# One hybrid block on one core: down sums added to the residual at once, modulation loads moved, T4 halves packed two to a tile

## The chip, the cores and the metric

The kernel runs on one core of a Trainium2 chip. The metric is the device time of one execution in microseconds; the number quoted for a kernel is the median of its runs. A profile is one further execution, with its own time.

## The reference

One layer (DEPTH is 1) of a diffusion backbone block. 512 latent tokens and 256 context tokens of width 2048; the output is the latent stream after a final RMSNorm. Cut to what matters:

```python
mod = (c_act @ w_mod + b_mod)                        # 2048 x 12288
sh1, sc1, gt1, sh2, sc2, gt2 = split(mod, 6)
h  = rmsnorm(x, g_norm1) * (1 + sc1) + sh1           # the same for ctx
lat_in, lat_gates = project_heads(h, w_in, ...)      # 4 GLA heads, 4 mLSTM heads
(lat_gla, lat_ml) = recurrent_groups(lat_in, ctx_in) # both directions
x = x + gt1 * merge_groups(lat_gla, lat_ml, lat_gates, ..., w_out)
h2 = rmsnorm(x, g_norm2) * (1 + sc2) + sh2
u_gate, u_val = split(h2 @ w_up, 2)                  # D_FF = 5504 each
g = conv3x3_depthwise(u_gate on an 8 x 64 grid) + conv_b
x = x + gt2 * ((silu(g) * u_val) @ w_down)
return rmsnorm(x, g_final)
```

Everything is in float32.

## The kernel before

The kernel is written in a tile framework: the program states operations on named tiles, and a planner places them on the engines' queues by priority (`tc.high_priority()`) and readiness, gives out buffers by tag and sets the semaphores. A tile asked for with a tag that is in use waits until the tile that had it has been read for the last time, wherever in the program that read stands. Blocks marked `pinned`, and single instructions marked `keep_in_program_order`, stay in the order of the program. Activations lie transposed, features on the partitions and 512 tokens along the free axis. Each float32 product is made of three matmuls of a high and a low part (`mm3`); every loaded weight tile is split for that by `split_new`: ACT casts `hi`, DVE subtracts to get `lo`. PE, DVE, ACT and the DMA queues run beside each other.

The stages in order:

1. `project_first`: the norm, the first two of the six modulation regions, and the projections of the first two heads.
2. For each head `h`, `weave` runs the stages of head `h` between the projection steps of head `h + 1` (`project_steps`). At the end of the last GLA head, while the first mLSTM head (index `H`, 4) is projected, `ml_gates` computes the gate rows of all mLSTM heads: a chain of small matmuls, DVE scans and the total `cum`, which PE then transposes into `pa`.
3. The four gates (`unit` on `w_gates`, tiles `ga`), then `w_out` (tiles `wo`), in 8 steps `kp` each. The new residual `x2` is also stored to DRAM tiles `x2d`.
4. The MLP in 11 groups `q` of `QUADS` (3, then ten times 4) blocks of 128 features. For each group: `up_gate`, `convolve`, `up_val`, and one group later `down_sums`, four blocks of 512 outputs each.
5. The last group's down blocks, the final norm and the output.

**Modulation fillers.** Regions 2 to 5 of the modulation vector (four totals `n` each, 16 in all) are computed on DVE, in `mod_chunk`: one load of 512 KB on SP's queue and two DVE instructions, eight chunks to a total; `mod_sums` and `mod_end` close a total with small pinned matmuls on PE (tiles `mr`, `mc`). These are put in a list `fillers`; every weight load calls `fill()`, which adds `rate[0]` to a credit and runs as many fillers as it allows. All must have run by the end of `w_out`. `project_steps` sets the rate to 2 from step 3 for heads `h >= H`; the first gate has 1.5; the rest of the gates and `w_out` have 2.0.

**The groups 1 to 10** use a two-by-two product in seven multiplications (`seven`, `four`). It needs sums of token halves: `token_sums(j)` makes, from the pair of tiles `x2[2j]` and `x2[2j+1]`, the operands `bt` (three halves), and leaves a fourth difference, T4, in a half of one of the two tiles. `token_last(j)` later splits that T4 into `bq[j][:, 1, :]`, which is the space of a half of `h2` that group 0, computed without the sums, still reads to the end of its `up_val`. The `x2` tiles have the tags `y0` to `y15`, and these tags are used again: by the convolutions `cv` of group 0, by the products `gh`, `gl` that go into the down blocks, and by `u`, `v`, `t` in `four` and `up_val`.

**Down sums.** A block's four sums go through ACT into a tile `st` (three buffers) and from there by a GpSimd-issued DMA to DRAM, accumulating there. With `FOLD = NQ - 3 = 8`, the groups up to 8 go unscaled into a separate total `dacc`, the first of them as plain stores. After the down blocks of group 8, `fold()` loads each of the 16 tiles of `dacc`, scales it on ACT by the gate `modc[5]` and adds it to `x2d`. Group 9 is scaled when it is copied and goes straight to `x2d`; group 10 is added on chip.

The order of the calls at the start of stage 4:

```python
for j in reversed(range(3, KP)):
    token_sums(j)
up_val(0, convolve(0))
for j in range(3):
    token_sums(j)
for j in range(KP):
    token_last(j)
down_sums(0, (0, 1), True)
```

Names as the profile has them: `ug`, `uv`, `dn`, `dl` are the accumulators of `up_gate`, `up_val`, the down blocks and the last ones; `hi_d` and `lo_d`, `hi_aug`, `hi_bug`, `hi_auv`, `hi_buv` and their `lo` are the split weights; `sum_m` is a modulation total, and `raw_...` a loaded weight tile.

Of the kernel before, what the change touches and what calls it, by code (L numbers as in the profile page):

```python
# [11 lines left out]
F32 = mybir.dt.float32  # L12
F32R = mybir.dt.float32r
U8 = mybir.dt.uint8
AF = mybir.ActivationFunctionType
ALU = mybir.AluOpType
PSUM = bass.MemoryType.PSUM

P = 128
HW = 256  # L20
D = 2048
KT = D // P
KP = KT // 2
T = 512
# [3 lines left out]
H = 4  # L28
# [8 lines left out]
LEVELS = [1, 2, 4, 8, 16, 32, 64]  # L37
QUADS = [3] + [4] * 10
NQ = len(QUADS)
FOLD = NQ - 3  # L40
GLA_COLS = {"q": 0, "k": 512, "v": 1024, "g": 2048, "lr": 3072}
ML_COLS = {"q": 3088, "k": 3600, "v": 4112, "g": 5136, "lr": 6160}

# [28 lines left out]
def block_kernel(ctx: ExitStack, tc: tile.TileContext, a: dict, out: bass.AP):  # L72
    nc = tc.nc
    V, S, G, PE = nc.vector, nc.scalar, nc.gpsimd, nc.tensor

    def pool(stack, name, bufs=1, space=None, waits="pool"):
        if space is None:
            return stack.enter_context(tc.tile_pool(name=name, bufs=bufs, reuse_waits=waits))
        return stack.enter_context(tc.tile_pool(name=name, bufs=bufs, space=space, reuse_waits=waits))

    def sub(o, x, y):
        V.tensor_tensor(out=o, in0=x, in1=y, op=ALU.subtract)  # L82
# [7 lines left out]
    def split(hi, lo, x):  # L90
        S.copy(hi, x)  # L91
        return V.tensor_tensor(out=lo, in0=x, in1=hi.bitcast(F32), op=ALU.subtract).ins  # L92
# [24 lines left out]
    modc = {n: keep.tile([P, KT], F32, name=f"mod{n}") for n in (2, 3, 4, 5)}  # L117
# [24 lines left out]
    def acc(name, shape=(P, T)):  # L142
        return (banks8[0] if banks8 else psA).tile(list(shape), F32, name=name, tag="acc")
# [5 lines left out]
    def ytile(k, name, shape=(P, T), dtype=F32):  # L149
        return yp.tile(list(shape), dtype, name=name, tag=f"y{k}")  # L150
# [14 lines left out]
    fillers = []  # L165
    rate, credit = [0], [0]
# [21 lines left out]
    def load_split(src, name, n=2, w=512):  # L188
        raw = load_raw(src, name, n, w)
        with tc.high_priority():  # L190
            parts = split_new(raw, name, (n, w))
        fill()
        return parts
# [34 lines left out]
    def unit(src, name, xh, xl, n=4, late=False, rates=None):  # L228

        accs = [acc(f"{name}_{i}") for i in range(n)]  # L230
        for _ in unit_steps(src, name, xh, xl, accs, late, rates):
            pass
        return accs
# [130 lines left out]
    def project_steps(h, banks):  # L364

        for kp in range(KP):
            rate[0] = 2 if h >= H and kp >= 3 else 0
            wh, wl = load_split(a["w_heads"][h, kp], f"h{h}_{kp}")
            for g in range(6):
                project_chunk(kp, wh, wl, banks[g], g)  # L370
                yield (1.36, 1.36, 1.44, 1.44, 1.04, 1.04)[g]
# [122 lines left out]
    cv = xp.tile([P, 32], F32, name="cv")  # L494
# [76 lines left out]
    for c0, n, hs, m in ((0, T, hx, gm[0]), (T, TC, hc, gm[1])):  # L571
        ps = psb(f"gm{c0}", (P, n))
        for k in range(KT):
            g = 32 * (k % 4)
# [417 lines left out]
    for h in range(1, 2 * H):  # L992
        if h + 1 < 2 * H:
            accs = [acc(f"a{h + 1}_{g}", BANKS[g]) for g in range(6)]
            steps = project_steps(h + 1, accs)
        else:
            rate[0] = 1.5
            accs = [acc(f"ga0_{i}") for i in range(4)]
# [12 lines left out]
    gp = pool(st_3, "gp", 2)  # L1011
    rp = pool(st_3, "rp")
    mod_raw.append(pool(st_3, "mraw3", 4, waits="tile"))
    rate[0] = 2.0
    for g in range(4):
        if g:
            accs = unit(a["w_gates"][g], f"ga{g}", *hx)
        for i in range(4):
            k = 4 * g + i
# [50 lines left out]

    dram = ctx.enter_context(tc.tile_pool(name="dram", bufs=1, space=bass.MemoryType.DRAM))
    x2d = [dram.tile([P, T], F32, name=f"x2d{k}", tag=f"x{k}") for k in range(KT)]
    dacc = [dram.tile([P, T], F32, name=f"dacc{k}", tag=f"d{k}") for k in range(KT)]
    sums2 = []
    for n in range(4):
        pinned[0] = n == 3
        accs = unit(a["w_out"][n], f"wo{n}", yh, yl)
# [9 lines left out]
        _, r2 = token_rstd(sums2, rp, "rms2", idle=4)  # L1087
        idle_products(acc("idle", (P, P)), sums2[0][:, 0:P], 7)
    pinned[0] = False
    print("LEFT", len(fillers))  # L1090
    assert not fillers
    st_3.close()
    st_h.close()
# [7 lines left out]
    stp = pool(ctx, "stp", 3, waits="tile")  # L1101
# [4 lines left out]
    def flat(x):  # L1106
        return x.rearrange("p a b -> p (a b)")

    bq = [[operand(j, part, "q", f"bq{part}{j}", (P, 4, HW)) for j in range(KP)] for part in "hl"]
# [10 lines left out]
    def half(k, i):  # L1120
        return x2[k][:, HW * i : HW * i + HW]

    def token_sums(j):

        k0, k1 = 2 * j, 2 * j + 1
        for k in (k0, k1):
            S.activation(x2[k], x2[k], AF.Identity, bias=modc[3][:, k : k + 1])
        sub(half(k0, 0), half(k0, 1), half(k0, 0))
        sub(half(k0, 1), half(k0, 1), half(k1, 1))
        sub(half(k1, 1), half(k1, 1), half(k0, 0))  # L1130
        sub(half(k1, 0), half(k1, 1), half(k1, 0))
        split(flat(bt[0][j][:, 0:2, :]), flat(bt[1][j][:, 0:2, :]), x2[k0])
        split(bt[0][j][:, 2, :], bt[1][j][:, 2, :], half(k1, 1))

    def token_last(j):

        split(bq[0][j][:, 1, :], bq[1][j][:, 1, :], half(2 * j + 1, 0))

    cwt = fp.tile([P, NF, 9], F32, name="cwt")
    cbt = fp.tile([P, 152], F32, name="cbt")[:, 0:NF]  # L1140
# [52 lines left out]
    def convolve(q):  # L1193
        convs = []
        for i in range(QUADS[q]):
            f = first_f(q) + i
            t = ytile(8 + i if q == 0 else 8 + 2 * i, f"cv{f}")
            t3 = t.rearrange("p (r c) -> p r c", c=GW)
            for tap in range(9):
                src = pads[:, i, tap // 3 : tap // 3 + ROWS, tap % 3 : tap % 3 + GW]  # L1200
                w = cwt[:, f, tap : tap + 1]
                if tap == 0:
                    S.activation(t3, src, AF.Identity, scale=w, bias=cbt[:, f : f + 1])  # L1203
                else:
                    V.scalar_tensor_tensor(out=t3, in0=src, scalar=w, in1=t3, op0=ALU.mult, op1=ALU.add)  # L1205
            S.activation(t, t, AF.Silu)
            convs.append(t)
        return convs

    def up_val(q, convs):  # L1210

        def product(i):
            if q == 0:
                gh, gl = (ytile((11, 12, 13, 14, 15, 7)[2 * i + n], f"g{p}{i}", dtype=F32R) for n, p in enumerate("hl"))
            elif q == NQ - 1:
                gh, gl = (operand(4 + i, p, "t", f"g{p}{first_f(q) + i}", (P, T)) for p in "hl")
            else:
                gh, gl = (ytile(2 * i + n, f"g{p}{first_f(q) + i}", dtype=F32R) for n, p in enumerate("hl"))
            split(gh, gl, convs[i])
            gs[first_f(q) + i] = (gh, gl)  # L1220

        if q == 0:
            accs = unit(a["w_up3"][1], "uv0", *h2, n=3)
            with tc.high_priority():
                for i, ps in enumerate(accs):
                    mul(convs[i], convs[i], ps)
                    product(i)
        else:
            def put(mh, th, x, ps, op):
                t = ytile(13, f"t{q}_{mh}{th}", (P, 2, HW))  # L1230
                V.tensor_tensor(out=t, in0=x, in1=ps, op=op)  # L1231
                for i in range(2):
                    c = convs[2 * mh + i][:, HW * th : HW * th + HW]
                    mul(c, c, t[:, i, :])
                if (mh, th) in ((1, 1), (0, 1)):
                    for i in range(2):
                        product(2 * mh + i)

            four(seven(a["w_up4"][2 * q - 1], f"uv{q}"), f"uv{q}", put)
# [16 lines left out]
    def down_sums(q, blks, by_f=False):  # L1256

        for blk in blks:
            accs = down_block(q, blk, by_f and blk == blks[0])
            with tc.high_priority():  # L1260
                for i in range(4):
                    k = 4 * blk + i
                    t = stp.tile([P, T], F32, name=f"st{q}_{k}", tag="st")
                    S.activation(t, accs[i], AF.Copy, scale=modc[5][:, k : k + 1] if q > FOLD else 1.0)  # L1264
                    if q == 0:
                        nc.gpsimd.dma_start(dacc[k], t)
                    else:
                        nc.gpsimd.dma_start(x2d[k] if q > FOLD else dacc[k], t, accum_op=ALU.add)  # L1268

    def fold():  # L1270

        for k in range(KT):
            t = stp.tile([P, T], F32, name=f"fold{k}", tag="st")
            nc.gpsimd.dma_start(t, dacc[k])
            S.activation(t, t, AF.Copy, scale=modc[5][:, k : k + 1])
            nc.gpsimd.dma_start(x2d[k], t, accum_op=ALU.add)

    up_gate(0)
    st_p.close()
    banks8.append(pool(ctx, "psM", 8, PSUM, waits="tile"))  # L1280
    for j in reversed(range(3, KP)):
        token_sums(j)
    up_val(0, convolve(0))
    for j in range(3):
        token_sums(j)
    for j in range(KP):
        token_last(j)
# [1 line left out]
    for q in range(1, NQ):  # L1289
        up_gate(q)  # L1290
        down_sums(q - 1, (2, 3) if q == 1 else range(3) if q == NQ - 1 else range(4))
        if q - 1 == FOLD:
            fold()
        up_val(q, convolve(q))
    down_sums(NQ - 2, (3,))

# [1 line left out]
    q = NQ - 1  # L1298
# [16 lines left out]
    for blk in range(3):  # L1315
        accs = down_block(q, blk)
# [38 lines left out]
    for hf, sl in enumerate(halves):  # L1355
        accs = [acc(f"dl{hf}_{i}", (P, T // 2)) for i in range(4)]
# [3 lines left out]
        for at, (n, i) in enumerate(order):  # L1360
# [5 lines left out]
            gh, gl = gs[fs[n]]  # L1366
# [76 lines left out]
```

## Time and profile before

| what | us |
|---|---|
| median of 3 runs | 2571.09 |
| lowest and highest run | 2570.16, 2573.83 |
| the profiled execution's own time | 2568.5 |
| its span | 2566.8 |
| PE busy in the span | 2487.4 |
| DVE busy | 1816.0 |
| ACT busy | 1021.1 |
| mean granted TensorE clock | 0.989 |

How to read the profile: the span runs from the first to the last instruction of the program. Engines are PE (matmul), PEld (weight load, beside PE), DVE, ACT, POOL and SP. A group's row has the line of the kernel, the engine, the operation, what it writes and reads, the count, then busy time, mean ns of one, and the idle time before it with what ended it. A row of waits reads "who waited <- for whom: us in total, times, longest". A row of windows has the stretch (us from the start of the span), its length, busy time of each engine with the count, the granted clock as a share of full speed, the mean busy share of the 16 DMA engines, and GB/s. Ends of matmuls are modelled, so a busy PE is not PE at its peak.

### The profile page before, as it was taken

Reading aid. Unit: us, or ns where it says so; the run is one execution under the profiler, and the core shown is the slowest. Engines: PE = TensorE matmul, PEld = TensorE weight load, DVE = VectorE, ACT = ScalarE, POOL = GpSimd, SP = SyncE. Lnnn points to the kernel's source line nnn. Section 1 sums busy time; section 2 is a strip of 40 time slices with the busy share of each in tenths; the row PEclk is TensorE's granted clock in tenths of the full one; section 3 lists DMA queues with packets and bytes.
Section 4 is the critical chain, followed back from the end, with each engine's and each line's share of the span. In section 5 each row is a group of like instructions: output and inputs, shape, how many; then the busy total and the mean of one; then the engine's idle time right before and its main releaser. Section 6 shows DMA issues by size and latency. Waiting matters only on the chain. (4 is left out here: it accounts for less than half of the span.)

```text
span 2566.8 us, 39444 instructions
## 1 busy us (share of the span) xinstructions
PE 2487.4 (97%) x15740; PEld 2218.3 (86%) x15740; DVE 1816.0 (71%) x2880; ACT 1021.1 (40%) x1530; POOL 200.5 (8%) x274
## 2 busy tenths in 40 slices
PE   6999999999999999999899999999999999998898
PEld 4887899788987888888798999999999999987897
DVE  6566764644446877749679787878787878784786
ACT  4225543322223233227344444444444444443445
POOL 0000000000000000000000101010111101014022
PEclk9999999999999999999999999999999999998999
DMA  9741111323334878732343736464655555468474
GB/s 384 266 166 34 34 42 42 123 83 107 115 124 159 281 270 303 255 128 89 123 136 95 168 109 163 112 155 122 148 128 143 132 140 135 128 150 198 117 193 132
DMA packets 124113, 380.59 MB, mean 148 GB/s; under 512 B 14421, under 2 KB 18841, under 8 KB 123929
## 3 DMA queue, kind: packets, MB, share of 16 engines
q1 hardware_dynamic: 94680, 318.29, 36.9%
q0 software_dynamic: 28160, 58.73, 12.3%
q8 instruction: 123, 2.02, 0.3%
q10 hardware_dynamic: 1088, 1.05, 0.1%
q14 instruction: 62, 0.50, 0.1%
HBM read 323.49 MB, written 54.53 MB: 147 GB/s over the span
## 5 line engine op out<-in xcount | busy, mean ns | idle before, releaser
L97 PE MATMUL dn<-gh,hi_d 128*128 128x512 f32 x672 | 262.2, 390 | 11.0 <-ACT gh L91 11.0
L97 PE MATMUL dn<-gl,hi_d 128*128 128x512 f32 x672 | 262.3, 390 | 0.0
L97 PE MATMUL dn<-gh,lo_d 128*128 128x512 f32 x672 | 262.0, 390 | 0.0
L1205 DVE SCALAR_TENSOR_TENSOR cv<-pads,cwt,cv 128x512 f32<-128x512 f32 x344 | 239.6, 744 | 1.1 <-ACT cv L1203 0.3
L305 DVE SCALAR_TENSOR_TENSOR sum_m<-raw_m,csil,sum_m 128x512 f32<-128x512 f32 x240 | 179.9, 750 | 8.7 <-DMA raw_m<-in_w_mod 3.2
L92 DVE TENSOR_TENSOR lo_buv<-sum_uv,hi_buv 128x1024 fp32r<-128x1024 f32 x80 | 97.9, 1223 | 122.3 <-ACT hi_buv L91 122.3
L1268 POOL DMA_DIRECT2D dacc<-st x128 | 111.8, 922 | 886.9 <-ACT st L1264 884.0
L97 PEld LDWEIGHTS dn<-gh,hi_d 128*128 128x128 f32 x672 | 126.6, 188 | 37.6 <-ACT gh L91 11.4
L97 PE MATMUL a<-hi_h,hTh 128*128 128x256 f32 x512 | 151.0, 295 | 0.5 <-ACT e L398 0.5
L97 PEld LDWEIGHTS dn<-gh,lo_d 128*128 128x128 f32 x672 | 126.4, 188 | 26.7 <-DVE lo_d L92 0.5
L97 PEld LDWEIGHTS dn<-gl,hi_d 128*128 128x128 f32 x672 | 126.5, 188 | 26.5 <-DVE gl L92 0.8
L97 PE MATMUL ug<-bth,hi_bug 128*128 128x256 f32 x480 | 137.3, 287 | 8.5 <-DVE u_uv L82 7.1
L97 PE MATMUL a<-lo_h,hTh 128*128 128x256 f32 x512 | 145.3, 284 | 0.0
L97 PE MATMUL a<-hi_h,hTl 128*128 128x256 f32 x512 | 145.2, 284 | 0.0
L97 PE MATMUL uv<-bth,hi_buv 128*128 128x256 f32 x480 | 137.8, 287 | 6.4 <-ACT hi_buv L91 6.4
L97 PE MATMUL uv<-bqh,hi_auv 128*128 128x256 f32 x480 | 136.7, 285 | 3.4 <-ACT hi_auv L91 3.4
L97 PE MATMUL uv<-bth,lo_buv 128*128 128x256 f32 x480 | 137.9, 287 | 1.2 <-DVE lo_buv L92 1.2
L92 DVE TENSOR_TENSOR lo_d<-raw_d,hi_d 128x1024 fp32r<-128x1024 f32 x86 | 102.7, 1195 | 50.5 <-ACT hi_d L91 49.8
L91 ACT CAST hi_d<-raw_d 128x1024 fp32r<-128x1024 f32 x86 | 88.7, 1031 | 123.9 <-PE ug L97 71.1
L97 PE MATMUL uv<-btl,hi_buv 128*128 128x256 f32 x480 | 137.4, 286 | 0.0
L97 PE MATMUL uv<-bqh,lo_auv 128*128 128x256 f32 x480 | 136.8, 285 | 0.2 <-DVE lo_auv L92 0.2
L97 PE MATMUL ug<-bqh,hi_aug 128*128 128x256 f32 x480 | 136.1, 284 | 0.7 <-DVE t L1231 0.4
(384 smaller groups left out, 7408.6 us busy)
## 6 DMA issues: line engine op xcount, KB each, us to landing
raw_m<-in_w_mod SPq DMA_DIRECT2D x192, 512.0 KB, 5.0
raw_d<-in_w_down SPq DMA_DIRECT2D x82, 512.0 KB, 3.4
raw_ug<-in_w_up SPq DMA_DIRECT2D x80, 512.0 KB, 3.6
raw_uv<-in_w_up SPq DMA_DIRECT2D x80, 512.0 KB, 5.2
dacc<-st POOLq DMA_DIRECT2D x144, 256.0 KB, 5.3
raw_h<-in_w_heads SPq DMA_DIRECT2D x64, 512.0 KB, 3.6
raw_ga<-in_w_gates SPq DMA_DIRECT2D x32, 512.0 KB, 4.2
raw_wo<-in_w_out SPq DMA_DIRECT2D x32, 512.0 KB, 4.6
```

What stands on the lines that cost most here:

```text
L91: S.copy(hi, x)
L92: return V.tensor_tensor(out=lo, in0=x, in1=hi.bitcast(F32), op=ALU.subtract).ins
L97: ins = PE.matmul(*args, **kw)
L305: V.scalar_tensor_tensor(out=parts[0], in0=x, scalar=ck, in1=parts[0], op0=ALU.mult, op1=ALU.add)
L1205: V.scalar_tensor_tensor(out=t3, in0=src, scalar=w, in1=t3, op0=ALU.mult, op1=ALU.add)
L1268: nc.gpsimd.dma_start(x2d[k] if q > FOLD else dacc[k], t, accum_op=ALU.add)
```

## The change

Three edits.

1. `FOLD`, `dacc` and `fold()` go. Every group's down sums are scaled by `modc[5]` on ACT and added to `x2d` in DRAM by an accumulating DMA, the first group's too.
2. `project_steps` runs fillers for `h > H` in place of `h >= H`: ten fillers fewer while the first mLSTM head is projected. From the second gate to the end of `w_out` the rate is 2.2 in place of 2.0.
3. T4 of pair `j` is kept in `rest(j)`, a half of tile `4 * (j // 2) + 2`, so that two of them share one tile (2, 6, 10 and 14), in place of a half of tile `2j + 1`. The convolutions of group 0 take tiles 8, 9 and 13 in place of 8, 9 and 10; its products take 11, 12, 15, 7, 4 and 5 in place of 11, 12, 13, 14, 15 and 7. `token_sums(2)` comes between `convolve(0)` and `up_val(0)`, and of the others 1 comes before 0.

```diff
-FOLD = NQ - 3
...
-            rate[0] = 2 if h >= H and kp >= 3 else 0
+            rate[0] = 2 if h > H and kp >= 3 else 0
...
-    rate[0] = 2.0
+    rate[0] = 2.2
...
-    dacc = [dram.tile([P, T], F32, name=f"dacc{k}", tag=f"d{k}") for k in range(KT)]
...
+    def rest(j):
+
+        return half(4 * (j // 2) + 2, j % 2)
+
     def token_sums(j):
...
-        sub(half(k1, 0), half(k1, 1), half(k1, 0))
         split(flat(bt[0][j][:, 0:2, :]), flat(bt[1][j][:, 0:2, :]), x2[k0])
+        sub(rest(j), half(k1, 1), half(k1, 0))
         split(bt[0][j][:, 2, :], bt[1][j][:, 2, :], half(k1, 1))
 
     def token_last(j):
 
-        split(bq[0][j][:, 1, :], bq[1][j][:, 1, :], half(2 * j + 1, 0))
+        split(bq[0][j][:, 1, :], bq[1][j][:, 1, :], rest(j))
...
-            t = ytile(8 + i if q == 0 else 8 + 2 * i, f"cv{f}")
+            t = ytile((8, 9, 13)[i] if q == 0 else 8 + 2 * i, f"cv{f}")
...
-                gh, gl = (ytile((11, 12, 13, 14, 15, 7)[2 * i + n], f"g{p}{i}", dtype=F32R) for n, p in enumerate("hl"))
+                gh, gl = (ytile((11, 12, 15, 7, 4, 5)[2 * i + n], f"g{p}{i}", dtype=F32R) for n, p in enumerate("hl"))
...
-                    S.activation(t, accs[i], AF.Copy, scale=modc[5][:, k : k + 1] if q > FOLD else 1.0)
-                    if q == 0:
-                        nc.gpsimd.dma_start(dacc[k], t)
-                    else:
-                        nc.gpsimd.dma_start(x2d[k] if q > FOLD else dacc[k], t, accum_op=ALU.add)
-
-    def fold():
-
-        for k in range(KT):
-            t = stp.tile([P, T], F32, name=f"fold{k}", tag="st")
-            nc.gpsimd.dma_start(t, dacc[k])
-            S.activation(t, t, AF.Copy, scale=modc[5][:, k : k + 1])
-            nc.gpsimd.dma_start(x2d[k], t, accum_op=ALU.add)
+                    S.activation(t, accs[i], AF.Copy, scale=modc[5][:, k : k + 1])
+                    nc.gpsimd.dma_start(x2d[k], t, accum_op=ALU.add)
...
-    up_val(0, convolve(0))
-    for j in range(3):
+    convs = convolve(0)
+    token_sums(2)
+    up_val(0, convs)
+    for j in (1, 0):
         token_sums(j)
...
-        if q - 1 == FOLD:
-            fold()
```

More of the change, by code (lines that the diff above doesn't have):

```diff
@@ L1089, in block_kernel @@
     pinned[0] = False
-    print("LEFT", len(fillers))
     assert not fillers
```

## The prediction

> **What bounds the kernel now.** I read the page first, then PE's waits over the whole span, then the stretches where PE idles.
>
> ```profile
> span 2566.8 us, 39444 instructions
> PE 2487.4 (97%) x15740; PEld 2218.3 (86%) x15740; DVE 1816.0 (71%) x2880; ACT 1021.1 (40%) x1530; POOL 200.5 (8%) x274
> PEclk9999999999999999999999999999999999998999
> ...
> PE dn L97 <- ACT gh L91: 11.0, 1, 11.0
> PE ug L97 <- DVE u_uv L82: 8.7, 2, 7.1
> PE uv L97 <- ACT hi_buv L91: 6.4, 2, 3.9
> PE pa L102 <- DVE cum L88: 3.9, 1, 3.9
> PE uv L97 <- ACT hi_auv L91: 3.4, 1, 3.4
> ```
>
> PE is busy for 97% of the span, and the change leaves its matmuls alone. What can be won is therefore the time in which PE waits, and the time after a wait in which its clock is granted below 1. Leaving aside the start, the five waits shown are the largest, and each lies at a place that the diff touches: `dn<-gh` in the first down block (the T4 edit), `pa<-cum` in `ml_gates` (the loads edit), and `uv<-hi_buv`, `uv<-hi_auv` and `ug<-u_uv` (7.1 of its 8.7) beside `fold`. So I price each place by comparing the stage with the same stage where nothing waits.
>
> **The fold.** These are windows cut at PE's first and last matmul of a stage: `uv` of group 8, `uv` of group 9 (just after `fold`), `ug` of group 9, `ug` of group 10. Columns: length, PE busy, granted clock, DMA share, GB/s. The waits under them are of the stretch 2290 to 2410.
>
> ```profile
> 2188.77:2229.25 40.48, 40.48 (x339) 1.00 0.46 117
> 2313.14:2372.29 59.15, 47.90 (x339) 0.86 0.87 195
> 2229.09:2269.76 40.67, 40.67 (x339) 1.00 0.32 104
> 2372.12:2423.30 51.18, 43.09 (x339) 0.93 0.41 115
> ...
> ACT fold L1275 <- DMA fold<-dacc: 37.0, 11, 6.2
> DVE lo_buv L92 <- ACT hi_buv L91: 26.9, 7, 7.5
> ```
>
> The same number of matmuls takes 59.15 instead of 40.48 and 51.18 instead of 40.67: 18.67 + 10.51 = 29.2 us. The cause is in the rows: ACT takes its instructions in order, and waits 37.0 us for loads of the separate total; behind these stand the casts `hi_buv` that feed the weight splits, and, at the end, the copy that `u_uv` starts from. Part of the loss is clock (0.86 and 0.93). The diff deletes all of it: 16 loads, 16 activations, 16 accumulating stores. What is late next there is nothing that I can see: `uv` of group 8 has the same down blocks ahead of it, with the same accumulating stores, and no wait. I take the whole 29.2.
>
> What replaces it: every `st` now has the scale of `modc[5]`.
>
> ```profile
> L1264 ACT ACTIVATE st<-dn x144: 579/600/604, 1245.6 to 2316.2; 128x512 f32<-128x512 f32 x144
> L1264 ACT ACTIVATE st<-dn,mod x16: 677/690/693, 2430.2 to 2509.1; 128x512 f32<-128x512 f32 x16
> ```
>
> That is 90 ns more for each of 144, 13 us on an engine busy for 40%, in fours: 0.36 us per down block. ACT's idle time beside a block hides it; without that cover it would be 13 us. The scale itself is there in time, since all modulation work ends before the up-projection. The stores to `x2d` of different groups lie a whole group apart, so the wait of an add for the add before it on the same tile costs nothing.
>
> **The first down blocks.** `dn` of group 0 comes in two pairs of blocks with the same matmuls. Then DVE's convolution taps (all of them, and two rows of the one that runs last), and the engines (PE, PEld, DVE, ACT, POOL, clock, DMA) in `uv` of group 0, the first pair, and `ug` of group 1.
>
> ```profile
> 1226.05:1255.74 29.69, 18.71 (x75) 0.83 0.41 141
> 1295.89:1312.73 16.84, 16.80 (x76) 1.00 0.63 211
> ...
> L1205 DVE SCALAR_TENSOR_TENSOR cv<-pads,cwt,cv 128x512 f32<-128x512 f32 x344 | 239.6, 744 | 1.1 <-ACT cv L1203 0.3
> 1222.70 1.54 DVE L1205 SCALAR_TENSOR_TENSOR cv<-pads,cwt,cv 128x512 f32<-128x512 f32 x2 [0.28 <-ACT cv L1203]
> 1234.98 3.10 DVE L1205 SCALAR_TENSOR_TENSOR cv<-pads,cwt,cv 128x512 f32<-128x512 f32 x4
> ...
> 1158.00:1226.00 68.00, 66.64 (x298) 55.04 (x298) 67.34 (x121) 49.77 (x81) 0.00 (x0) 1.00 0.26 82
> 1226.00:1255.74 29.74, 18.76 (x75) 14.53 (x75) 16.51 (x25) 10.52 (x16) 2.97 (x6) 0.83 0.41 141
> 1255.57:1296.05 40.48, 40.48 (x338) 40.47 (x337) 24.89 (x34) 14.77 (x18) 1.52 (x3) 1.00 0.32 105
> ```
>
> The first pair loses 29.69 - 16.84 = 12.85 us, 11.0 of it one wait for `gh`. One convolution starts only at 1222.70, since its tile (y9) holds a T4 half until `token_last` has written it into the space of `h2`, which `uv` reads to its end. The new `rest` keeps all T4 halves in tiles 2, 6, 10 and 14, and the convolutions take 8, 9 and 13, which are free by the time the taps can run. So the third convolution moves ahead of `uv`'s end, and `token_sums(1)`, `token_sums(0)` and the `token_last` move behind it.
>
> Is there room on DVE? Before 1226 it is full (67.34 of 68), and of the late convolution's 8 taps the first 2 run before 1226, so 6 taps moved ahead (6 x 0.744 = 4.5 us) push as much other work behind. Behind, 16.51 us of work would stand in 16.84 us: just full, then 15.6 us free in `ug`. What is queued behind the moved sums is the split of the first `ug` weights, and PE waits for that. Bounds: 0, if the order lets the splits go first, to 3 us, one such set of splits late. I take 1.0, nearer to 0, as `ug` needs the sums of one pair per 5 us only.
>
> The other cost is DMA. The first 16 stores were plain and now add. The software queue's rows of 1240 to 1320 (16 plain) and 1400 to 1450 (16 adding), then the landing times, plain and adding:
>
> ```profile
> q0 software_dynamic: 1268, 4.20, 14.3%
> q0 software_dynamic: 2304, 4.20, 53.6%
> DMA to landing us min/median/max: 2.3/4.2/7.0
> DMA to landing us min/median/max: 3.8/5.4/10.9
> ```
>
> One plain store takes 0.143 x 80 / 16 = 0.72 us of all 16 engines, one that adds 0.536 x 50 / 16 = 1.68; 8 of them per pair add 7.7 us. The first pair then needs 0.41 x 29.69 + 7.7 = 19.9 us of DMA in 16.84, the second 0.63 x 16.84 + 7.7 = 18.3: 3.1 and 1.5 us overdue. There are 3 `st` buffers, so a late landing holds ACT, and behind it the casts for the next weights. Upper bound 3.1 + 1.5, plus 1.2 of later landing at each pair: 7.0 us. Lower bound 0, since the loads that compete are partly for a stage with a share of 0.32 and can slip; below 0 is excluded, an add being the dearer in both rows. I take the middle, 3.5. [...]
>
> Sum: 12.85 - 1.0 - 3.5 = 8.35 us.
>
> **The modulation loads.** `h > H` takes 10 chunks (20 DVE instructions, 10 loads of 512 KB on SP) out of the stage in which `ml_gates` runs; they move into the stretch of gates and `w_out`, where the rate goes from 2.0 to 2.2. First DVE between 486 and 515, then PE's second wait there, then the same engine columns as above.
>
> ```profile
> L305 DVE SCALAR_TENSOR_TENSOR sum_m<-raw_m,csil,sum_m 128x512 f32<-128x512 f32 x12 | 9.0, 748 | 2.3 <-DMA raw_m<-in_w_mod 2.1
> PE pgc L97 <- DVE dg L866: 1.1, 2, 0.9
> 510.00:515.00 5.00, 1.09 (x11) 0.90 (x10) 4.96 (x6) 0.60 (x1) 0.00 (x0) 0.80 0.42 116
> 515.00:520.00 5.00, 4.06 (x23) 3.73 (x22) 3.36 (x8) 0.27 (x2) 0.00 (x0) 0.52 0.73 257
> ```
>
> These 12 stand between the links of a chain that DVE runs for `cum`, for which PE waits 3.9 us. 9.0 us out of that chain is more than twice the wait, so it goes, with 0.9 of `pgc`. The clock then is not lowered: 4.06 x 0.48 + 1.09 x 0.20 = 2.2 us. Together 7.0 us. After it nothing is late in that stage but waits of 0.3. [...]
>
> Where they go to:
>
> ```profile
> 815.00:1095.00 280.00, 280.00 (x1305) 228.20 (x1304) 213.09 (x296) 82.74 (x110) 6.82 (x9) 1.00 0.77 268
> DVE sum_m L303 <- PE mr L311: 25.4, 7, 3.7
> raw_m<-in_w_mod SPq DMA_DIRECT2D x81, 512.0 KB, 5.2
> q1 hardware_dynamic: 21313, 72.59, 74.9%
> ```
>
> PE is busy for all of the 280 us. 20 instructions at 0.75 us bring DVE from 213 to 228 us; 10 loads at 0.749 x 280 / 72.59 x 0.524 = 1.5 us bring the DMA share from 0.77 to 0.83. On SP each stands ahead of weight loads, which are four buffers ahead. Bounds of the cost: 0 (both below full) and 15 us (DVE full). Nothing can be won, as PE does not wait. I take 0: the share moves by a twentieth.
>
> **Sum.** 29.2 + 8.35 + 7.0 = 44.5 us. The profiled execution took 2568.5 us (its span, 2566.8, and 1.7 around it), so 2524.0; the median of the runs, 2571.09, lies 2.6 above, so 2526.6, which I give as 2526.5.
>
> **Rivals.** (1) The convolution is no longer late, but PE only waits a little further on: DVE, full up to 1243, and the adding stores make `ug` of group 1 late, and the convolutions of group 1 after it, a stretch which is tight already:
>
> ```profile
> 1352.88:1399.00 46.12, 42.52 (x339) 40.98 (x338) 44.05 (x69) 17.34 (x22) 0.00 (x0) 1.00 0.24 81
> ```
>
> There `ug` of group 2 takes 46.12 instead of 40.67 with DVE at 44 of 46. For it: that row. Against it: DVE's 15.6 free microseconds in `ug` of group 1, in between. All 8.35 us would go: 2535.
>
> (2) `cum` is not what holds `pa`: without the loads the chain still has its three weight splits and four scans, and PE waits as long. Against it: 9.0 of 29 us of DVE's time there. 7.0 us would go: 2533.5.
>
> (3) The edit does not do what it says for the fold, because the group after it waits for adding stores instead of for loads, and half of 29.2 stays: 2541. Against it: group 8, with the same stores, has no wait.
>
> (4) Slower. The small matmuls `mr`, which close each modulation total, stand in a fixed place in PE's order. If DVE falls behind in gates and `w_out`, PE waits at each of the 12 totals that are closed there (16 in all, 4 closed by then) for one chunk to land, 5.2 us: 62 us, 18 more than the gain, 2589. It decides from the point at which DVE has no slack, 67 us of 280 now and 52 after. Against it: DVE waits for `mr` there (25.4 us), so it is ahead of PE, not behind.
>
> **How the numbers follow.** Forecast 0.65, (1) 0.14, (2) 0.10, (3) 0.06, (4) 0.05. The best end has no cost at the first blocks: 29.2 + 12.85 + 7.0 = 49.1, 2522.0; with the runs' spread below the median (0.9) and some of the wait in `ug` of group 2 gone, 2518. The other end holds (1), (2) and both together (2542) and most of (3): 2543. What lies above is (4) and fold's share beyond half. A measurement of this kernel tells about 0.2%, 5 us, from no change; all cases but (4) are faster by more, and I leave 0.01 for mishaps that cancel: faster 0.94, same 0.01, slower 0.05.
>
> **What would show it.** Right: no `fold` and no wait for it; `uv` of group 9 at 40.5 and `ug` of group 10 at 40.7; the first `dn` pair near 17 to 20 us with all 24 taps before `uv` ends; no `pa<-cum` wait, clock 1.00 at 500 to 550; PE still without waits from gates to `w_out`. Wrong: `st` holding ACT for microseconds around the first four blocks and PE waiting for `hi_bug` or `hi_buv` there, as in (1); PE waiting at `mr`, as in (4).

## The result and the profile after

| | before | after |
|---|---|---|
| median of four runs, us | 2571.32 | 2524.98 |
| lowest and highest | 2570.16, 2573.83 | 2524.58, 2525.8 |
| span of the profiled execution | 2566.8 | 2523.1 |
| mean granted clock | 0.989 | 0.997 |

The ratio of the changed kernel's time to that of the kernel before is 0.9819, with a 95% interval of 0.9802 to 0.9836. The forecast was 2526.5, with a range of 2518 to 2543. The profiled execution took 2524.79, against 2524.0 in the sum.

The head of the page of the changed kernel, its row for the evictions, and PE's waits over the whole span:

```profile
span 2523.1 us, 39365 instructions
PE 2474.2 (98%) x15740; PEld 2207.8 (88%) x15740; DVE 1815.5 (72%) x2880; ACT 1023.7 (41%) x1514; POOL 182.8 (7%) x242
...
L1265 ACT ACTIVATE st<-dn,mod 128x512 f32<-128x512 f32 x160 | 108.6, 689 | 120.6 <-DMA x2d<-st 92.0
...
PE ss_l L96 <- DVE sq_l L87: 19.3, 1, 19.3
PE sl L96 <- DVE ex L84: 2.4, 3, 1.3
PE dn L96 <- ACT st L1265: 2.3, 1, 2.3
PE ug L96 <- ACT st L1265: 2.2, 2, 1.7
...
PE ug L96 <- DVE u_uv L81: 1.6, 1, 1.6
PE uv L96 <- ACT pads L1185: 1.4, 1, 1.4
```

PE issues the same 15740 matmuls, POOL 32 instructions fewer (the 16 loads and 16 stores of `fold`), ACT 16. The five waits of the prediction's first fence are gone, except for 1.6 us of `ug<-u_uv`. Two waits are new: `dn<-st` and `ug<-st`, 4.5 us together. PE waits there for ACT to empty an accumulator into a tile `st`.

The windows of PE answer to those of before. In this order: first `dn` pair, `ug` of group 1, second `dn` pair, `ug` of group 2, `uv` of group 9, `ug` of group 10. Columns: length, PE busy, granted clock, DMA share, GB/s.

```profile
1217.39:1234.07 16.68, 16.68 (x75) 1.00 0.63 180
1233.90:1278.49 44.59, 42.35 (x338) 0.96 0.50 123
1278.33:1297.80 19.47, 17.14 (x76) 1.00 0.71 185
1337.94:1384.02 46.08, 42.49 (x339) 1.00 0.25 81
2298.23:2338.71 40.48, 40.48 (x339) 1.00 0.46 117
2338.54:2379.21 40.67, 40.67 (x339) 1.00 0.32 104
```

Against before: 29.69 to 16.68 (-13.0), 40.48 to 44.59 (+4.1), 16.84 to 19.47 (+2.6), 46.12 to 46.08, and in the last two 59.15 to 40.48 and 51.18 to 40.67 (-29.2).

The stage of `ml_gates` and the long stretch of gates and `w_out`, all engines (PE, PEld, DVE, ACT, POOL, clock, DMA share, GB/s), and DVE's wait for `mr` in that stretch:

```profile
510.00:515.00 5.00, 5.00 (x43) 4.85 (x42) 1.76 (x8) 1.18 (x5) 0.00 (x0) 1.00 0.29 105
515.00:520.00 5.00, 5.00 (x31) 4.49 (x30) 2.76 (x7) 1.40 (x3) 0.00 (x0) 1.00 0.16 40
800.00:1085.00 285.00, 285.00 (x1332) 232.03 (x1331) 227.17 (x322) 83.10 (x113) 6.83 (x9) 1.00 0.81 280
DVE sum_m L302 <- PE mr L310: 15.9, 7, 3.7
```

PE is busy throughout at full clock in all three. Followed matmul by matmul, the one that stood at 520.53 now stands at 511.82: 8.71 us earlier. 0.82 of that is already there from 250 to 490, in a stretch that the change does not touch, so the stage itself gave 7.9.

The table of where the 43.7 us of span went:

| place | predicted | measured |
|---|---|---|
| `uv` of group 9, `ug` of group 10 | -29.2 | -29.2 |
| first `dn` pair | -12.85 | -13.0 |
| given back in the stages after it | +4.5 | +6.7 |
| `ml_gates` | -7.0 | -7.9 |
| moved modulation loads | 0 | 0 |

The rows of the table sum to -43.4; the rest is scatter of some tenths, such as the 0.82 above.

### The profile page after: what moved, and what is told of

It is laid out like the page before. It is cut to its first block, busy times and chain, and to the rows that moved or that the text cites. A ratio compares the mean times of both kernels' runs of the same rounds, so it can differ in the third digit from the quotient of the medians.

```text
span 2523.1 us, 39365 instructions
## 1 busy us (share of the span) xinstructions
PE 2474.2 (98%) x15740; PEld 2207.8 (88%) x15740; DVE 1815.5 (72%) x2880; ACT 1023.7 (41%) x1514; POOL 182.8 (7%) x242
## 4 chain that ended last, share of the span: by engine, by line
PE 90%; DVE 4%; issue 3%; DMA 2%; ACT 1%; POOL 0%; SPq 0%; DVEq 0%; POOLq 0%; ACTq 0%
PE a L96 19%; PE dn L96 17%; PE uv L96 16%; PE ug L96 15%; PE ga L96 7%; PE wo L96 7%; PE po L96 4%; PE sl L96 1%; PE ps_m L96 1%; DMA raw_m<-in_w_mod 1%; PE cst L96 1%; PE s L96 1%; DVE cv L1206 0%; DMA xl<-in_xT 0%; DVE sum_ug L87 0%
## 5 line engine op out<-in xcount | busy, mean ns | idle before, releaser
L1266 POOL DMA_DIRECT2D x2d<-st x160 | 140.3, 916 | 1153.7 <-ACT st L1265 1149.4
L304 DVE SCALAR_TENSOR_TENSOR sum_m<-raw_m,csil,sum_m 128x512 f32<-128x512 f32 x240 | 180.0, 750 | 10.4 <-DMA raw_m<-in_w_mod 4.5
L1265 ACT ACTIVATE st<-dn,mod 128x512 f32<-128x512 f32 x160 | 108.6, 689 | 120.6 <-DMA x2d<-st 92.0
L96 PE MATMUL ug<-bql,hi_aug 128*128 128x256 f32 x480 | 136.1, 284 | 0.0
L96 PE MATMUL ug<-bqh,lo_aug 128*128 128x256 f32 x480 | 136.1, 284 | 0.0
```

Source lines behind the costliest of these rows:

```text
L96: ins = PE.matmul(*args, **kw)
L304: V.scalar_tensor_tensor(out=parts[0], in0=x, scalar=ck, in1=parts[0], op0=ALU.mult, op1=ALU.add)
```

## Experiments

In the two later comparisons the kernel before ran at 2574.4 and 2574.5, some 3 us above the first, so each ratio is to the runs of the kernel before that stood beside it, and the lengths of stages in the traces are the finer measure.

### The parts alone

**The fold alone** (before, with only this edit):

```diff
-S.activation(t, accs[i], AF.Copy, scale=modc[5][:, k : k + 1] if q > FOLD else 1.0)
...
+S.activation(t, accs[i], AF.Copy, scale=modc[5][:, k : k + 1])
+nc.gpsimd.dma_start(x2d[k], t, accum_op=ALU.add)
...
-            fold()
```

> Only the first edit: no dacc, no fold, every group's sums scaled and added to x2d. Theory (the fold edit alone earns the 29 us in groups 9 and 10, and gives some 6 us back at the first four down blocks, because their stores now add and hold ACT and the accumulators): uv of group 9 at 40.5 us, ug of group 10 at 40.7, and a loss of 3 to 7 us against the kernel before around the first four down blocks; total 23 to 26 us faster, about 2546. Rival (what is given back there comes from the T4 edit's order on DVE): nothing is lost at the first down blocks, 29 us faster, about 2542.

Measured: 2545.89, ratio 0.9885 (0.9868 to 0.9901), so 25.5 to 34 us faster. Its windows, first `dn` pair, `ug` of group 1, second pair, `uv` of group 9, `ug` of group 10:

```profile
1228.35:1259.65 31.30, 19.90 (x75) 0.78 0.48 127
1259.49:1299.97 40.48, 40.48 (x338) 1.00 0.50 110
1299.81:1319.63 19.82, 17.41 (x76) 1.00 0.69 184
2320.16:2360.63 40.47, 40.47 (x339) 1.00 0.49 117
2360.47:2401.14 40.67, 40.67 (x339) 1.00 0.34 104
```

The last two rows give the whole 29.2 back. Rival (3), by which half of it would stay as a loss, falls. The adding stores of group 0 cost 1.6 in the first pair, where they lie beside the old wait, and 3.0 in the second. By its stages the net is 24.6, a little under the interval of the runs.

**The loads alone**:

```diff
-            rate[0] = 2 if h >= H and kp >= 3 else 0
+            rate[0] = 2 if h > H and kp >= 3 else 0
...
-    rate[0] = 2.0
+    rate[0] = 2.2
```

> Only the second edit: ten modulation chunks moved out of the stage of ml_gates, rate 2.2 later. Theory (the chunks' DVE instructions stand in the chain for cum): the wait pa<-cum goes, 7 to 9 us faster, about 2563, and PE has no new wait in gates and w_out. Rival (the gain before 1150 us in the changed kernel came with the other edits' replanning): under 3 us.

Measured: 2563.65, ratio 0.9955 (0.9941 to 0.997), 7.7 to 15 us. PE's waits from 476 to 531, all that are left, and the stretch of gates and `w_out`:

```profile
PE pre L97 <- ACT yT L643: 0.3, 1, 0.3
...
800.00:1085.00 285.00, 285.00 (x1333) 232.00 (x1332) 227.16 (x321) 84.14 (x114) 6.83 (x9) 1.00 0.82 282
```

Both `pa<-cum` and `pgc<-dg` are gone (7.9 us by PE's matmuls from 490 to 521), and the stretch that took the loads in has PE busy for all of its 285 us. Rival (2) falls by the first line, rival (4) by the second.

**T4 alone**, the stores of group 0 still plain (edit 3 of the change and nothing else):

```diff
-        sub(half(k1, 0), half(k1, 1), half(k1, 0))
+        sub(rest(j), half(k1, 1), half(k1, 0))
...
-            t = ytile(8 + i if q == 0 else 8 + 2 * i, f"cv{f}")
+            t = ytile((8, 9, 13)[i] if q == 0 else 8 + 2 * i, f"cv{f}")
```

> Only the third edit: T4 two to a tile, with the other tiles and the order of token_sums. The first group's stores stay plain stores to dacc. Theory (the late convolution was the whole of the 11.0 us wait, and the moved token sums cost nothing): first dn pair at 17 us, ug of group 1 at 40.5, 12 to 13 us faster, about 2558.5. Rival (the moved token sums make ug of group 1 late on DVE): ug of group 1 at 43 to 45, 8 to 10 us faster.

Measured: 2561.35, ratio 0.9946 (0.993 to 0.9962), 10 to 18 us. First pair, `ug` of group 1, second pair:

```profile
1226.94:1244.13 17.19, 16.87 (x75) 1.00 0.64 197
1243.97:1284.45 40.48, 40.48 (x338) 1.00 0.38 126
1284.28:1301.34 17.06, 16.90 (x76) 1.00 0.63 201
```

The first pair gains 12.5, and nothing is given back behind it: `ug` of group 1 has 40.48 as before. The DVE work that this edit moves behind `uv` therefore costs nothing.

### What gives the gain back

The stages after the first pair lose 6.7 us when T4 is packed and the stores add, 3.0 with the adding stores alone and 0.2 with T4 alone. Two things could do it: the adds load the DMA engines, so that weights come late; or each add holds its `st` buffer longer, so that ACT can't empty accumulators.

**Plain stores in group 0**, the rest as in the changed kernel (a plain store overwrites the residual, so this kernel leaves it out):

```diff
-                    nc.gpsimd.dma_start(x2d[k], t, accum_op=ALU.add)
+                    if q == 0:
+                        nc.gpsimd.dma_start(x2d[k], t)
+                    else:
+                        nc.gpsimd.dma_start(x2d[k], t, accum_op=ALU.add)
```

> The changed kernel with plain stores to x2d for group 0, so that the residual is left out of the sum: it shows the time without the adding DMAs of the first four blocks. Theory (the adding stores hold ACT there): ug of group 1 back to 40.5 and the second dn pair back to 16.9; 5 to 6.5 us below the changed kernel, about 2519. Rival (DVE's moved work): within 1 us of the changed kernel, 2525.

Measured: 2518.42, ratio 0.978 (0.9763 to 0.9796); by medians 6.6 us under the changed kernel. Same three windows:

```profile
1216.85:1233.97 17.12, 16.93 (x75) 1.00 0.61 211
1233.81:1274.29 40.48, 40.48 (x338) 1.00 0.37 120
1274.12:1291.22 17.10, 17.05 (x76) 1.00 0.64 206
```

So the adds are all of it, 6.0 by these stages. It does not yet tell DMA from buffers. The changed kernel's trace leans to the buffers: its ACT timeline from the first pair on (start, length, instruction, in brackets the idle time before it and what ended it), and below that PE's matmuls that waited.

```profile
1224.65 1.83 ACT L1265 ACTIVATE st<-dn,mod 128x512 f32<-128x512 f32 x3
...
1231.51 0.69 ACT L1265 ACTIVATE st<-dn,mod 128x512 f32<-128x512 f32 x1 [4.51 <-DMA x2d<-st]
...
1234.86 0.69 ACT L1265 ACTIVATE st<-dn,mod 128x512 f32<-128x512 f32 x1 [1.42 <-DMA x2d<-st]
...
1237.46 0.69 ACT L1265 ACTIVATE st<-dn,mod 128x512 f32<-128x512 f32 x1 [1.91 <-DMA x2d<-st]
...
1240.13 0.69 ACT L1265 ACTIVATE st<-dn,mod 128x512 f32<-128x512 f32 x1 [1.98 <-DMA x2d<-st]
...
1238.20 0.39 PE L96 MATMUL ug<-bth,hi_bug 128*128 128x256 f32 x1 [0.55 <-ACT st L1265]
1240.87 0.58 PE L96 MATMUL ug<-bqh,hi_bug 128*128 128x256 f32 x1 [1.68 <-ACT st L1265]
```

The first three evictions fill the three buffers at once. Before the fourth, ACT stands for 4.51 us until an add has landed, and before each of the next three for one more landing. PE, which wants these accumulators for `ug`, starts 0.05 us after the ends of the evictions of 1237.46 and 1240.13.

**More `st` tiles, same adds**: nine of group 0's sixteen `st` go to `y` tiles that are free at that time.

```diff
+                    free = {3: 13, 4: 8, 5: 3, 6: 1, 7: 0, 11: 13, 12: 0, 13: 2, 14: 6}.get(k) if q == 0 else None
-                    t = stp.tile([P, T], F32, name=f"st{q}_{k}", tag="st")
+                    if free is None:
+                        t = stp.tile([P, T], F32, name=f"st{q}_{k}", tag="st")
+                    else:
+                        t = ytile(free, f"st{q}_{k}")
```

> The changed kernel with nine of group 0's sixteen st tiles in y tiles that are free at that time, so that ACT can empty the accumulators without waiting for a store to land. The stores still add. Theory (the give-back is ACT waiting for one of three st buffers, not the DMA engines being late with weights): ug of group 1 back to 40.5 and the second dn pair to about 17; 5 to 6.5 us below the changed kernel, about 2519. Rival (the adding stores fill the DMA engines, so that weight loads land late whatever the buffers): within 2 us of the changed kernel, 2523 to 2525, with PE waiting for split weights instead.

Measured: 2516.12, ratio 0.9775 (0.9761 to 0.979), 8.9 us under the changed kernel by medians. First pair, `ug` of group 1, second pair, `ug` of group 2; then the landing times of group 0's stores, in the changed kernel and in this one:

```profile
1216.40:1233.22 16.82, 16.82 (x75) 1.00 0.63 180
1233.06:1273.53 40.47, 40.47 (x338) 1.00 0.52 135
1273.37:1290.32 16.95, 16.89 (x76) 1.00 0.62 174
1330.47:1374.34 43.87, 41.84 (x339) 1.00 0.26 85
```

```profile
DMA to landing us min/median/max: 3.7/5.5/10.4
DMA to landing us min/median/max: 4.3/6.7/10.6
```

The adds are the same and land even later (6.7 against 5.5), and yet 4.1 and 2.5 us come back, and 2.2 more in `ug` of group 2: the give-back was the wait for a buffer, not the DMA engines. An estimate from these rows fits: two blocks of four sums take 16.68 us, and three buffers, each taken for 0.69 + 5.5 us, serve 3 x 8.34 / 6.2 = 4.0 sums in the time of a block, just the four that it has, with nothing in reserve. With the plain stores' 0.60 + 4.2 it was 5.2. In later groups, with four features to a block instead of three, ACT still waits for landings (92.0 us in the whole span, of which 16.2 lie between 1217 and 1300), but PE waits for no `st`. That fits with a longer block, but was not tried.

**What was left of the wait in `ug` of group 2**: on top of the last edit, `v` of group 1 and its third convolution go to tiles that are free earlier.

```diff
-        u, v = ytile(9, f"u_{name}", (P, 2, HW)), ytile(11, f"v_{name}", (P, 2, HW))
+        u, v = ytile(9, f"u_{name}", (P, 2, HW)), ytile(3 if name == "ug1" else 11, f"v_{name}", (P, 2, HW))
...
-            t = ytile((8, 9, 13)[i] if q == 0 else 8 + 2 * i, f"cv{f}")
+            t = ytile((8, 9, 13)[i] if q == 0 else 1 if q == 1 and i == 2 else 8 + 2 * i, f"cv{f}")
```

> The version with e5's st tiles, and in group 1 with v in tile 3 and one convolution in tile 1, in place of 11 and 12, which hold a product of group 0 until its last down block is done. Theory (ug of group 2 takes 46.1 in place of 40.7 because the convolutions of group 1 start only when tile 11 is free, at the end of the second dn pair): ug of group 2 near 40.7, about 5 us below e5, about 2514. Rival (DVE is simply short of time in group 1, whenever the convolutions start): ug of group 2 at 44 or more, within 2 us of e5.

Measured: 2512.54, ratio 0.9761 (0.9746 to 0.9775), faster than both kernels: 12.5 us less than the 2525.02 of the next experiment, which ran beside it with the changed kernel's time. `ug` of group 1, second pair, `ug` of group 2:

```profile
1234.26:1274.74 40.48, 40.48 (x338) 1.00 0.53 136
1274.57:1291.08 16.51, 16.51 (x76) 1.00 0.67 172
1331.23:1372.38 41.15, 41.08 (x339) 1.00 0.34 102
```

`ug` of group 2 goes from 46.08 in the changed kernel to 43.87 with the `st` tiles and to 41.15 here. The run gains 3.6 us on the last experiment, less than the 5 expected, which counted from 46.1. The excess that the prediction put down to a DVE that is nearly full (44 us of 46) was largely the convolutions of group 1 starting late for want of a tile: their taps start at 1280.3 here, at 1295.9 with the `st` tiles alone, and at 1305.7 in the changed kernel, and DVE is now busy for 35.5 of the 41.15 us. The two tiles were moved together, so what each is worth is open.

### Which half of a modulation chunk holds `ml_gates`

A chunk is a load and two DVE instructions. Each is put back alone into the stage that the change cleared: ten loads of 512 KB that nobody reads, or twenty DVE instructions on data that is there.

```diff
+            if h == H and kp >= 3:
+                for i in range(2):
+                    nc.sync.dma_start(mod_tile(f"raw_x{kp}_{i}"), a["w_mod2"][0, i, kp])
```

> The changed kernel with ten loads of 512 KB put back on SP's queue into the stage of ml_gates, at the places where the kernel before had the chunks; nothing reads them and no DVE instruction is added. Theory (the chunks' DVE instructions delayed cum): no wait pa<-cum, within 1.5 us of the changed kernel, 2524 to 2526.5. Rival (the loads delayed the head's weights, and with them the projections and the splits): 4 us or more slower, 2529 or above.

```diff
+            if h == H and kp >= 3:
...
+                for i in range(4):
+                    with tc.issue_after(parted[0]):
...
+                            V.scalar_tensor_tensor(out=jk, in0=cst[:, 0:T], scalar=csil[:, i : i + 1], in1=jk,
+                                                   op0=ALU.mult, op1=ALU.add)
```

> The changed kernel with twenty DVE instructions of 128 x 512 put back into the stage of ml_gates, behind the weight splits as the chunks were, on a tile that is already on chip; no loads are added, and nothing uses the result. Theory (these instructions delay cum): the wait pa<-cum is back with 3 to 4 us and the clock is halved after it; 6 to 8 us above the changed kernel, about 2532. Rival (the loads): 2525.

Measured: the loads alone 2525.02, ratio 0.9809 (0.9795 to 0.9824), no different from the changed kernel; the DVE instructions alone 2532.85, ratio 0.9839 (0.9822 to 0.9855). PE's waits from 476 to 531, loads alone first, then DVE alone, with the latter's windows:

```profile
PE pre L96 <- ACT yT L645: 0.3, 1, 0.3
```

```profile
PE pgc L96 <- DVE dg L875: 2.5, 1, 2.5
...
510.00:515.00 5.00, 2.44 (x14) 0.76 0.21 56
515.00:520.00 5.00, 5.00 (x28) 0.50 0.13 51
520.00:525.00 5.00, 5.00 (x23) 0.72 0.00 0
```

DVE's time in the chain is enough to bring back nearly the whole loss (7.2 of 7.9 us by PE's matmuls from 486 to 526, 7.8 by medians), and the loads are worth nothing by themselves. The wait stood at `pgc<-dg` here and not at `pa<-cum`, another link of the same chain, so the expectation was right in the cause and wrong in the place.

## Why the prediction was right, point by point

- **The median, 2526.5**: that it came within 1.5 us of the measured 2524.98 is partly luck. The stages gave 43.4 us where the sum had 44.5. The prediction then added 2.6 us for the distance of the median from the profiled execution; in the changed kernel that distance is 0.2.
- **The fold, 29.2**: exact for the profiled execution, and shown by the fold alone. Ordinary stages of the same shape, without a wait, were the right measure of what a stage would fall to. What they cost with `fold` varies: `uv` of group 9 and `ug` of group 10 with the loads alone, then with T4 alone, which both keep `fold`, lose 31.1 and 32.1 us (rows below, columns as in the windows of PE above). A distance of some 3 us between median and profiled execution could come from there, but only one execution of each kernel has a trace.

```profile
2306.71:2367.77 61.06, 47.95 (x338) 0.86 0.88 189
2367.61:2418.84 51.23, 42.97 (x339) 0.93 0.44 116
2302.36:2362.69 60.33, 46.80 (x337) 0.92 0.86 187
2363.02:2415.92 52.90, 44.27 (x337) 0.87 0.44 114
```

- **The scale on every `st`, 0**: 160 of 689 ns now, and `uv` of group 9 and `ug` of group 10 are at their full pace with it. Only in group 0 is the eviction on PE's path, and there for its buffer, not for its 90 ns.
- **The first pair, 12.85**: 13.0. All taps are done by 1210.1, ahead of the first matmul of `dn` at 1217.39.
- **DVE, 1.0**: mis-sized; it is 0. The prediction took DVE's 16.51 us of work in 16.84 for a risk. In the changed kernel DVE is busy for 13.21 of 16.68 there, and `ug` of group 1 keeps 40.48 both with T4 alone and with plain stores.
- **The adding stores, 3.5**: mis-sized; 6.7, near the upper bound of 7.0. The prediction summed DMA time against the stage's length and took the middle. The first pair, for which it had 19.9 us of DMA in 16.84, lost nothing, at a DMA share of 0.63; the loss fell on `ug` of group 1 and the second pair. The buffers were named in it, but as a way by which weights would come late; the sum that decides is buffers against landing time, and PE waited for accumulators. Of what it called a sign of being wrong, the first half came (`st` held ACT for 4.51 us), the second, PE waiting there for `hi_bug`, did not. The two errors together moved the time by 2.2 us.
- **The modulation loads, 7.0**: 7.9. Waits were 5.5 rather than 4.8 (the small `pre<-li` and the second `pgc` went as well), which leaves 2.4 for the clock, against the 2.2 worked out from its rows.
- **The moved loads, 0**: PE busy for 285 of 285 us, DVE at 227 (the prediction had 228 of 280), DMA share 0.81 (predicted 0.83).
- **The rivals**: (1) is half right. `ug` of group 1 and the pair behind it took 6.7 of the 13.0 back, not all, and through ACT's buffers rather than through DVE. (2) falls by the loads alone and the two halves of a chunk, (3) by the fold alone, (4) because PE never waits for `mr`: DVE still waits for it, 15.9 us instead of 25.4, so it stays ahead of PE with less in hand.

## What to carry to other kernels

When a store becomes an accumulating store, count the buffers behind it against its landing time, not only its bytes against the DMA engines: a queue of three that had kept pace with plain stores (median landing 4.2 us) became the bound with adding ones (5.5 us), and nine borrowed tiles ended it (8.9 us by medians). A wait that is removed is measured best by a sister stage without it. A filler between the links of a serial chain cost by its engine time there (7.8 us by medians for the twenty DVE instructions); its loads cost nothing here, at a DMA share of 0.48 with them put back.

## What was not expected of the hardware

The clock fell without one long pause. These are windows of the changed kernel in `ug` of group 1 (PE, PEld, DVE, ACT, POOL, clock, DMA share, GB/s): a stretch around two short waits, and the 3.41 us that follow.

```profile
1237.65:1240.87 3.22, 0.98 (x8) 0.78 (x7) 0.00 (x0) 1.24 (x3) 0.86 (x1) 0.95 1.04 162
1240.56:1243.97 3.41, 3.10 (x14) 3.10 (x15) 2.15 (x3) 3.41 (x5) 1.76 (x2) 0.50 0.81 112
```

After waits of 0.55 and 1.68 us, with 0.98 us of matmuls in 3.22, the clock is 0.50 for 3.41 us, which makes up most of the 1.9 us that the stage lost beyond its 2.2 of waiting. A single wait of 2.27 us in the second pair left it at 1.00 (the row at 1278.33 above), and the 2.5 us wait of the DVE experiment halved it for about 10.2 us (the three windows from 510: 0.24, 0.50 and 0.28 of 5 us below full speed, doubled). Why the clock fell after two short waits here and not after the longer one of 2.27 us, no run settles.

Accumulating stores behind one another landed late: three issued back to back, at 1225.77 and 0.6 us apart, landed 5.6, 8.4 and 10.4 us after their issue. Three plain stores at the same place, in the experiment with plain stores, took 3.7, 5.4 and 6.4, so the adds landed 1.9, 3.0 and 4.0 us later. The 3.5 us that the prediction set against the adds were too few.
